# A planned encoder layer: tile places by end of last use, four rounds of planning, another transfer model

## The chip, the core and the metric

The kernel runs on one core of one Trainium2 chip. The metric is the device time of one execution in microseconds (us); before the change the median of three runs is 1985.77 us (1983.18 to 1986.04). Engines are named as in the profile: PE is TensorE, PEld its weight loads, DVE is VectorE, ACT is ScalarE, POOL is GpSimd, SP is SyncE, which here issues nearly all DMAs.

## What is computed

The reference is one layer of an encoder, for 1024 tokens of one new stream and 32 tokens of a running one (1056 together), with 1024 channels, in float32:

```python
def swiglu(x, w_gate, w_up, w_down):
    return (jax.nn.silu(x @ w_gate) * (x @ w_up)) @ w_down

def layer(x, ...):
    x = x + 0.5 * rmsnorm(swiglu(rmsnorm(x, g1a), f1g, f1u, f1d), g1b)
    m, k_new, v_new, h_last, new_buf = mixer(rmsnorm(x, gma), ...)
    x = x + rmsnorm(m, gmb)
    x = x + 0.5 * rmsnorm(swiglu(rmsnorm(x, g2a), f2g, f2u, f2d), g2b)
```

The two feed-forward nets (FFN1, FFN2) have 2816 = 22 x 128 inner channels. The mixer projects to queries, keys, values and two inputs of a recurrent block. Four heads of differential attention (two score maps each; the running stream also sees 512 cached keys) stand beside a causal convolution with a gated linear recurrence (RG-LRU) over 512 channels; both results are concatenated and projected once more.

## The kernel before

**Tiling.** Every float32 factor is split into a high and a low part of the type fp32r (a cast and a subtraction, `split`), and a product is made of three matmuls (`mm3`): high by high, high by low, low by high. The FFNs run in three stages. *Gate and up*: 11 rounds, each for two of the 22 blocks of inner channels. A round loads two 512 KB tiles of gate weights (`raw<-in_w1g`; `in_w2g` in FFN2) and two of up weights (`raw<-in_w1u`), forms the sums that a Strassen-like scheme of seven products needs (`left_operands`, tiles `W`, `s`, `raw`), multiplies them with the tiles `X` into PSUM (`pq`), combines the products in tiles `p` and `u`, and stores combinations of the result `H` to DRAM (`t_d<-H`). *Down*: tiles `traw` come back from `t_d`, become `T`, and are multiplied with the down weights (`pd`, `pe`). *Boundary*: `rstd` gets the norm. The sums of squares `acc` are added over the partitions by matmuls (`st<-ones,acc`), GpSimd raises them to the power -0.5 (tile `ms`), and matmuls with the identity spread them (`st<-ident,ms`).

In the mixer `pp` are the products of the input projection, `xc` and `th` the convolution's tiles, `pg` the products of the gates of the recurrence, which DVE computes by scans (`th<-lx,xc`). `KS` holds the cached keys, split in two parts. `Sh0s` to `Sh3s` and `Sh0q` to `Sh3q` are scores of head 0 to 3 for the running and the new stream, `pth2q`, `tpsh2q` and `oh2q` are transposed weights and outputs of head 2, `cat` the concatenated result, which goes through DRAM (`cat_d`), and `po` the products of the output projection with its weights `w` (high) and `wl` (low).

**Places.** SBUF is not given out by names but by rings. A `Ring` is a row of equal places; `S`, the largest, has 45 places of 1064 floats and holds the raw weights, `W`, `X`, `u`, `H`, `T` and most of the mixer's tiles. Three more rings hold `tp`, `up` and `acc` tiles, five the tiny ones. Each new tile takes a place by `Planner.take`, and its first writer has to wait until all users of the place's former holder are done.

**Order.** The program is run once without issuing anything: every operation becomes an `Op` with the engines that may do it and a cost on each. `Planner.run` takes places and finds the dependences, and then makes 12 passes. In a pass, `forward` fills the engines in the order of priorities by a model of costs; in it all transfers share one channel, each taking its bytes divided by 360 per ns behind a start of 1150 ns, and being usable 900 ns after that. `backward` runs the same from the end and gives the priorities of the next pass. The pass with the shortest modelled time decides the order and, where several engines may do an operation, the engine. `pin` then fixes this order on every engine, and the program is run again and issued (L138 before, L142 after, is the line that issues everything, so all rows of the profile name it). On the chip each engine and SP's DMA queue work in that order, and an instruction that waits holds those behind it.

Of the kernel before, what the change touches and what calls it, by code (L numbers as in the profile page):

```python
# [29 lines left out]
LOUD = 0  # L30
# [18 lines left out]
class Planner:  # L49
# [6 lines left out]


    ENGINES = ("tensor", "vector", "scalar", "gpsimd", "sync")
    PASSES = 12

    def __init__(self, tc, plan=None):
        self.tc, self.plan = tc, plan
        self.made = []
        self.count = 0
        self.floor = 0.0
        self.hurry = 0.0
        self.top = 0
        self.held = []
        self.old = {}
        self.cells_of = {}  # L70
        self.last_use = {}
        self.events = []
        self.slots = []
        self.ops = []
        self.deps = []
        self.cells = {}
        self.touched = {}
        for e in self.ENGINES:
            setattr(self, e, EngineView(self, (e,)))
        self.adder = EngineView(self, ("vector",))  # L80
        self.copier = EngineView(self, ("scalar", "vector"), (0, 0))
        self.later = EngineView(self, ("vector",))
# [20 lines left out]
    def take(self, name, ring):  # L103


        now = len(self.deps)
        found = [(self.last_use.get(t, -1), j) for j, t in enumerate(ring.holds)]
        last, j = min(found)
        assert last < now, (ring.name, name)
        ring.holds[j] = name  # L110
        self.slots.append(j)
        _, space, lo = ring.slots[j]
        hi = lo + ring.size
        waits, keep = {}, []
        for sp, a, b, other in self.held:
            if sp == space and a < hi and lo < b:
                found = [u for cell in self.cells_of.get(other, ()) for users in self.cells[cell].values() for u in users]
                waits.update(dict.fromkeys(found) if found else self.old[other])
                keep += [(sp, *g, other) for g in ((a, lo), (hi, b)) if g[0] < g[1]]
            else:  # L120
                keep.append((sp, a, b, other))
        self.held = keep + [(space, lo, hi, name)]
        self.old[name] = waits
# [64 lines left out]
    def forward(self, prio):  # L188

        ops, n = self.ops, len(self.ops)  # L190
        left = [len(d) for d in self.deps]
        est = [op.floor for op in ops]
        end, start, chosen = [0.0] * n, [0.0] * n, [None] * n
        free = dict.fromkeys(self.ENGINES, 0.0)
        later = {e: [] for e in self.ENGINES}
        ready = {e: [] for e in self.ENGINES}
        order = {e: [] for e in self.ENGINES}
        dma, table, skip = 0.0, None, set()
        window, worked, cold = 0, 0.0, True

        def release(i):
            for e in ops[i].engines:
                heapq.heappush(later[e], (est[i], prio[i], i))

        for i in range(n):
            if not left[i]:
                release(i)
        todo = n
        while todo:
            best = None  # L210
            for e in self.ENGINES:
                q, r = later[e], ready[e]
                while r and chosen[r[0][1]] is not None:
                    heapq.heappop(r)
                while q and (q[0][0] <= free[e] or chosen[q[0][2]] is not None):
                    _, p, i = heapq.heappop(q)
                    if chosen[i] is None and (i, e) not in skip:
                        heapq.heappush(r, (p, i))
                t = free[e] if r else q[0][0] if q else None
                if t is not None and (best is None or t < best[0]):  # L220
                    best = (t, e)
            t, e = best
            q, r = later[e], ready[e]
            while q and q[0][0] <= t:
                _, p, i = heapq.heappop(q)
                if chosen[i] is None and (i, e) not in skip:
                    heapq.heappush(r, (p, i))
            if not r:
                continue
            p, i = heapq.heappop(r)  # L230
            if chosen[i] is not None:
                continue
            op = ops[i]
            if len(op.engines) > 1:
                k = op.engines.index(e)
                mine = t + op.costs[k] + op.bias[k]
                other = [max(free[o], est[i]) + op.costs[j] + op.bias[j] + sum(ops[x].cost(o) for _, x in ready[o][:8] if x != i and _ < p)
                         for j, o in enumerate(op.engines) if j != k and (i, o) not in skip]
                if other and min(other) < mine:
                    skip.add((i, e))  # L240
                    continue
            cost = op.cost(e)
            if e == "tensor":
                while t >= (window + 1) * GATE:
                    cold = worked < (0.8 if cold else 0.4) * GATE
                    window, worked = window + 1, 0.0
                cost *= 1 + cold
                worked += cost * (op.writes[0].free_size() > 1)
            if op.tables:
                if table not in op.tables:  # L250
                    table = op.tables[0]
                    cost += 1300
            chosen[i] = e
            start[i] = t
            free[e] = t + cost
            if op.size:
                dma = max(t + 1150, dma) + op.size / 360.0
                end[i] = dma + 900
            else:
                end[i] = t + cost  # L260
            order[e].append(i)
            todo -= 1
            for j, kind in self.after[i]:
                d = ops[j]
                if kind == ORDER:
                    x = start[i]
                elif op.size:
                    x = end[i]
                else:
                    x = end[i] + (0 if len(d.engines) == 1 and d.engines[0] == e and (e == "tensor" or kind == AGAIN) else LATENCY[e][d.engines[0]])  # L270
                est[j] = max(est[j], x)
                left[j] -= 1
                if not left[j]:
                    release(j)
        return chosen, start, end, order, max(end)

    def backward(self, prio, chosen):

        ops, n = self.ops, len(self.ops)
# [10 lines left out]
        while todo:  # L290
            best = None
            for e in self.ENGINES:
                q, r = later[e], ready[e]
                while q and q[0][0] <= free[e]:
                    _, p, i = heapq.heappop(q)
# [14 lines left out]
            for j, kind in self.deps[i].items():  # L310
                o = ops[j]
                if kind == ORDER:
                    x = t + cost - o.cost(chosen[j])
                elif o.size:
                    x = t + cost + o.size / 360.0 + 1600
                else:
                    x = t + cost + (0 if chosen[j] == e and (e == "tensor" or kind == AGAIN) else LATENCY[chosen[j]][e])
                est[j] = max(est[j], x)
# [2 lines left out]
                    heapq.heappush(later[chosen[j]], (est[j], prio[j], j))  # L321
        return at

    def run(self):
        for f, args in self.events:
            f(*args)
        n = len(self.ops)
        self.after = [[] for _ in range(n)]
        for i, deps in enumerate(self.deps):
            for j, kind in deps.items():  # L330
                self.after[j].append((i, kind))
        best = None
        prio = list(range(n))
        for k in range(self.PASSES):
            found = self.forward(prio)
            if LOUD:
                print("pass", k, found[4])
            if best is None or found[4] < best[0][4]:
                best = found, prio
            chosen, start = found[:2]  # L340
            prio = [-a - op.hurry for op, a in zip(self.ops, self.backward([-s for s in start], chosen))]
        best, _ = best
        self.chosen, self.start, _, self.order, _ = best
        self.ops = self.deps = self.after = self.cells = self.events = None

    def pin(self):
# [16 lines left out]
class Op:  # L363
    def __init__(self, engines, bias, name, args, kw, floor):
# [11 lines left out]
            self.bias = bias[:k] + bias[k + 1:]  # L376
        self.size, self.tables = 0, None
        if name == "dma_start":
            side = self.writes[0] if self.writes[0].space != bass.MemoryType.DRAM else self.reads[0]
            self.size = side.free_size() * side.shape[0] * 4  # L380
        elif name == "activation":
            self.tables = TABLES.get(args[2])
        self.costs = [engine_cost(e, self) for e in self.engines]
# [5 lines left out]
class Ring:  # L389


    def __init__(self, plan, stack, name, size, bufs, banks=None):
        self.plan, self.name, self.size = plan, name, size
        self.holds = [None] * (len(banks) if banks else bufs)
        if banks is not None:
            self.slots = banks
            return
# [1169 lines left out]
```

## Time and profile before

| | before |
|---|---|
| median of 3 runs | 1985.77 us (1983.18 to 1986.04) |
| the profiled execution's own time | 1988.15 us |
| its span, first to last instruction | 1986.4 us |
| mean granted clock of TensorE | 0.987 |
| PE / DVE / ACT / POOL busy | 1899.0 / 1444.8 / 642.5 / 70.1 us |
| bytes read / written in HBM | 157.48 / 65.83 MB |

The time of an execution is a little longer than the span of its instructions. A duration in the trace is that of the profiled execution. Matmuls of TensorE overlap, so the distance between their starts tells what one costs, not the duration of one.

### The profile page before, as it was taken

The page shows a single profiled execution, that of the slowest core. Times are in us where ns is not written, and L with a number is a line of the kernel's source. Part 1 is how long each engine was busy: PE and PEld are TensorE (multiplying, and loading weights), DVE is VectorE, ACT ScalarE, POOL GpSimd, SP SyncE. Part 2 cuts the span into 40 slices and gives each one's busy share as a digit, 9 for nine tenths or more (in the row PEclk, how much of TensorE's full clock was granted, in tenths as well). Part 3 has the DMA queues.
Part 4 walks back from the last instruction along what each step waited for, and adds up shares of the span by engine and source line. Part 5 has one row for each costly group of instructions (what it writes and reads, how often), then busy time and mean ns, then how long its engine had stood idle before and what let it go on. Part 6 is the DMA issues. An engine that isn't in the chain of part 4 may idle for free.

```text
span 1986.4 us, 35224 instructions
## 1 busy us (share of the span) xinstructions
PE 1899.0 (96%) x14456; PEld 1850.0 (93%) x14456; DVE 1444.8 (73%) x2649; ACT 642.5 (32%) x1259; POOL 70.1 (4%) x79
## 2 busy tenths in 40 slices
PE   5999999999999999997998899989999999999997
PEld 5999999999999999896987789989999999999997
DVE  7867677676789588257677868797677676778857
ACT  5311111113332144164377763341111211223212
POOL 2000000000000011002000010000000000000000
PEclk9999999999999999998999999989999999999998
DMA  3223233234554253242433432232233222464442
GB/s 131 82 92 92 87 119 98 90 94 154 178 164 137 82 160 100 78 141 92 129 89 103 127 120 86 88 103 92 87 118 98 88 96 82 159 208 142 148 120 88
DMA packets 127809, 225.60 MB, mean 114 GB/s; under 512 B 11424, under 2 KB 84896, under 8 KB 127648
## 3 DMA queue, kind: packets, MB, share of 16 engines
q1 hardware_dynamic: 127504, 223.31, 35.5%
q8 instruction: 113, 1.85, 0.4%
q14 instruction: 48, 0.39, 0.1%
q10 hardware_dynamic: 144, 0.05, 0.0%
HBM read 157.48 MB, written 65.83 MB: 112 GB/s over the span
## 4 chain that ended last, share of the span: by engine, by line
PE 72%; DVE 13%; DMA 8%; ACT 3%; issue 3%; POOL 1%; SPq 1%; POOLq 0%; DVEq 0%; ACTq 0%
PE pq L138 31%; PE pd L138 19%; PE pp L138 7%; PE pe L138 4%; PE po L138 4%; PE pv L138 3%; DVE W L138 2%; DVE H L138 2%; DMA raw<-in_w1u 2%; DVE raw L138 1%; DMA raw<-in_w2u 1%; PE st L138 1%; DVE y L138 1%; DMA t_d<-H 1%; DVE u L138 1%
## 5 line engine op out<-in xcount | busy, mean ns | idle before, releaser
L138 PE MATMUL pq<-X,W 128*128 128x264 f32 x7488 | 931.1, 286 | 18.9 <-DVE u L138 10.6
L138 PEld LDWEIGHTS pq<-X,W 128*128 128x128 f32 x7488 | 922.5, 190 | 24.6 <-DVE u L138 14.5
L138 PE MATMUL pd<-T,W 128*128 128x264 f32 x3024 | 368.7, 284 | 0.0
L138 PEld LDWEIGHTS pd<-T,W 128*128 128x128 f32 x3024 | 368.3, 188 | 0.0
L138 ACT CAST W<-raw 128x512 fp32r<-128x512 f32 (+1 forms) x226 | 133.8, 607 | 511.5 <-DVE raw L138 233.1
L138 DVE TENSOR_TENSOR W<-raw,W 128x512 fp32r<-128x512 f32 (+1 forms) x376 | 246.3, 670 | 13.9 <-ACT W L138 10.9
L138 DVE TENSOR_TENSOR u<-u,pq 128x528 f32<-128x528 f32 x80 | 56.3, 704 | 101.0 <-PE pq L138 100.5
L138 PE MATMUL pp<-xm,w 128*128 128x352 f32 x384 | 127.5, 332 | 0.8 <-ACT w L138 0.8
L138 PE MATMUL pp<-xm,wl 128*128 128x352 f32 x384 | 125.9, 328 | 0.0
L138 DVE TENSOR_TENSOR raw<-raw 128x512 f32<-128x512 f32 (+1 forms) x150 | 115.0, 772 | 4.8 <-DMA raw<-in_w1d 2.0
L138 DVE TENSOR_TENSOR u<-p,pq 128x528 f32<-128x528 f32 x80 | 56.2, 702 | 84.8 <-PE pq L138 84.8
L138 ACT CAST T<-traw 128x528 fp32r<-128x528 f32 x84 | 52.2, 634 | 172.9 <-DMA traw<-t_d 110.9
L138 DVE TENSOR_TENSOR T<-traw,T 128x528 fp32r<-128x528 f32 x126 | 85.8, 704 | 4.9 <-ACT T L138 3.5
L138 POOL TENSOR_TENSOR ms<-ms,neghalf 128x3 f32<-128x3 f32 x24 | 31.6, 1320 | 1518.2 <-DVE ms L138 1518.2
L138 DVE CAST W<-raw 128x512 fp32r<-128x512 f32 (+1 forms) x150 | 62.2, 416 | 28.4 <-ACT H L138 12.1
L138 DVE TENSOR_TENSOR acc<-acc,sq 128x264 f32<-128x264 f32 x167 | 69.6, 429 | 13.2 <-ACT sq L138 11.2
L138 PE MATMUL po<-cat,wl 128*128 128x264 f32 x256 | 73.3, 290 | 4.5 <-DVE wl L138 4.5
L138 PE MATMUL po<-cat,w 128*128 128x264 f32 x256 | 76.4, 303 | 1.0 <-ACT y L138 0.5
L138 PEld LDWEIGHTS pp<-xm,w 128*128 128x128 f32 x384 | 73.1, 190 | 2.6 <-ACT w L138 1.1
L138 PEld LDWEIGHTS pp<-xm,wl 128*128 128x128 f32 x384 | 72.9, 190 | 1.0 <-DVE wl L138 0.6
L138 PE MATMUL pe<-h,w 128*128 128x264 f32 x256 | 73.2, 286 | 0.0
L138 PE MATMUL pe<-hl,w 128*128 128x264 f32 x256 | 73.1, 286 | 0.0
(410 smaller groups left out, 2549.3 us busy)
## 6 DMA issues: line engine op xcount, KB each, us to landing
t_d<-H SPq DMA_DIRECT2D x126, 264.0 KB, 2.3
traw<-t_d SPq DMA_DIRECT2D x56, 528.0 KB, 3.9
raw<-in_w1g SPq DMA_DIRECT2D x22, 512.0 KB, 3.6
raw<-in_w1u SPq DMA_DIRECT2D x22, 512.0 KB, 4.2
raw<-in_w2u SPq DMA_DIRECT2D x22, 512.0 KB, 3.8
raw<-in_w2g SPq DMA_DIRECT2D x22, 512.0 KB, 3.6
raw<-in_w1d SPq DMA_DIRECT2D x36, 256.0 KB, 3.7
raw<-in_w2d SPq DMA_DIRECT2D x36, 256.0 KB, 3.5
```

What stands on the lines that cost most here:

```text
L138: self.made.append(f(*args, **kw).ins)
```

## The change

No operation of the computation is added, removed or resized. Three things change in the planner.

*Which place.* `take` took the place whose holder has its last use first in the order of the program text. Now the first of four rounds does that; in the next rounds it takes, among the places whose holder has no later use in the program, the one whose holder's last use ends earliest in the schedule that the former round found (`self.left`). Each round makes the places and the dependences anew (`replay`) and has 6 passes, and the best of all passes counts, together with its places (`slots`).

*Transfers.* One byte in the model takes 1/305 ns in place of 1/360, and 1.5 times that where the tile has at most 64 partitions, and again 1.5 times where the rows on the far side have at most 128 elements. A load is usable 1000 ns behind its last byte and a store 400 ns, where both had 900.

*Tables.* A table load of ACT counts 1410 ns in place of 1300.

```diff
-    PASSES = 12
+    ROUNDS, PASSES = 4, 6
...
         now = len(self.deps)
         found = [(self.last_use.get(t, -1), j) for j, t in enumerate(ring.holds)]
-        last, j = min(found)
-        assert last < now, (ring.name, name)
+        found = [(self.left.get(ring.holds[j], 0.0) if self.left else last, j) for last, j in found if last < now]
+        assert found, (ring.name, name)
+        j = min(found)[1]
...
-                    cost += 1300
+                    cost += 1410
...
-                dma = max(t + 1150, dma) + op.size / 360.0
-                end[i] = dma + 900
+                dma = max(t + 1150, dma) + op.moved
+                end[i] = dma + op.landing
...
-                    x = t + cost + o.size / 360.0 + 1600
+                    x = t + cost + o.moved + 700 + o.landing
...
+        for k in range(self.ROUNDS):
+            self.replay()
+            mine = None
+            for n in range(self.PASSES):
+                found = self.forward(prio)
...
+                if mine is None or found[4] < mine[4]:
+                    mine = found
...
+            if best is None or mine[4] < best[0][4]:
+                best = mine, self.slots
+            self.left = {}
+            for op, end in zip(self.ops, mine[2]):
+                for ap in op.reads + op.writes:
+                    self.left[ap.tensor.name] = max(end, self.left.get(ap.tensor.name, 0.0))
+            prio = mine[1]
...
-            side = self.writes[0] if self.writes[0].space != bass.MemoryType.DRAM else self.reads[0]
+            side, far = self.writes[0], self.reads[0]
+            self.landing = 1000
+            if side.space == bass.MemoryType.DRAM:
+                side, far, self.landing = far, side, 400
             self.size = side.free_size() * side.shape[0] * 4
+            self.moved = self.size / 305.0 * (1.5 if side.shape[0] <= 64 else 1) * (1.5 if far.ap[-1][1] <= 128 else 1)
```

What the diff doesn't tell is how the order moves. Three places show it.

SP's queue in the first rounds of FFN1's gate and up stage, before (behind the loads of the input `x`; the first round's weights are loaded ahead of these):

```order
L138 DMA x<-in_xt 128x2x264 x12
L138 DMA t_d<-H 128x2x264
L138 DMA raw<-in_w1u 128x1024
L138 DMA t_d<-H 128x2x264
L138 DMA raw<-in_w1u 128x1024
L138 DMA raw<-in_w1g 128x1024 x2
L138 DMA t_d<-H 128x2x264 x5
L138 DMA raw<-in_w1g 128x1024 x2
L138 DMA t_d<-H 128x2x264 x2
L138 DMA raw<-in_w1u 128x1024
L138 DMA t_d<-H 128x2x264
L138 DMA raw<-in_w1u 128x1024
```

The same place of SP's queue after:

```order
L142 DMA x<-in_xt 128x2x264 x12
L142 DMA raw<-in_w1g 128x1024
L142 DMA t_d<-H 128x2x264 x2
L142 DMA raw<-in_w1g 128x1024
L142 DMA raw<-in_w1u 128x1024 x2
L142 DMA t_d<-H 128x2x264 x5
L142 DMA raw<-in_w1g 128x1024 x2
L142 DMA raw<-in_w1u 128x1024
L142 DMA t_d<-H 128x2x264
L142 DMA raw<-in_w1u 128x1024
L142 DMA t_d<-H 128x2x264 x6
```

The second round's loads moved ahead of stores, and in the rounds that follow the first load of up weights stands next to the gate weights, and six stores follow each other where four and two stood.

DVE's order at the first use of the cached keys (`KS`) in the mixer, before:

```order
L138 TENSOR_TENSOR xc<-xc,th 128x1060
L138 SCALAR_TENSOR_TENSOR th<-a_9745,th 128x352
L138 SCALAR_TENSOR_TENSOR th<-lx,xc 128x1024
L138 SCALAR_TENSOR_TENSOR th<-lx,cst,xc 128x32
L138 TENSOR_TENSOR xc<-xc,th 128x1060 x3
L138 SCALAR_TENSOR_TENSOR th<-lx,xc 128x1024
L138 SCALAR_TENSOR_TENSOR th<-lx,cst,xc 128x32
L138 SCALAR_TENSOR_TENSOR th<-lx,xc 128x1024
L138 SCALAR_TENSOR_TENSOR th<-lx,cst,xc 128x32
L138 TENSOR_TENSOR KS<-u,KS 64x512
```

And after (the rows with `th<-lx` are the scans, long ones for the new stream and short ones for the running one):

```order
L142 TENSOR_TENSOR xc<-xc,th 128x1060
L142 SCALAR_TENSOR_TENSOR th<-a_9745,th 128x352
L142 SCALAR_TENSOR_TENSOR th<-lx,xc 128x1024
L142 CAST KS<-u 128x512
L142 SCALAR_TENSOR_TENSOR th<-lx,cst,xc 128x32
L142 SCALAR_TENSOR_TENSOR tq<-pp,rb 128x352
L142 CAST KS<-u 128x512
L142 TENSOR_TENSOR KS<-u,KS 64x512 x2
```

Two scan pairs and the three `xc` sums moved behind `KS`, and its casts moved from ACT to DVE. Between the last `pg` product and the first `Sh0s` PE has 92 `pp` products before and 76 after.

PE's order where the attention of head 2 ends and the output projection begins, before:

```order
L138 MATMUL Sh3s<-KS,Q 32x512
L138 MATMUL Sh3s<-KS,Ql 32x512
L138 MATMUL tpsh2q_11852<-ident,P0h2q_11839 128x128
L138 MATMUL tpsh2q_11852<-ident,P0h2q_11822 128x128
L138 MATMUL tpsh2q_11852<-ident,P0h2q_11839 128x128
L138 MATMUL tpsh2q_11861<-ident,P0h2q_11839 128x128 x2
L138 MATMUL po<-cat_11996,w 128x264
```

And after:

```order
L142 MATMUL Sh3q_12190<-K,Q 128x512
L142 MATMUL Sh3q_12190<-K,Ql 128x512
L142 MATMUL Sh3q_12198<-K,Q 128x512
L142 MATMUL Sh3q_12198<-K,Ql 128x512
L142 MATMUL Sh3q_12198<-K,Q 128x512
L142 MATMUL po<-cat_11996,w 128x264
L142 MATMUL po<-cat4l,w 128x264
L142 MATMUL Sh3q_12198<-K,Ql 128x512
```

Scores of head 3 moved ahead of the first `po`. From the last `pp` to the first `po` there are 36 matmuls before and 61 after, and of the `po` products 310 before and 256 after stand ahead of the last output of head 3. At FFN2's entry the last norm's sums stand 93 `pq` products behind the norm ahead of it before and 114 after, and 3 and 16 `pq` products lie between its sums and its `st<-ident,ms`.

## Rows read from the trace of the kernel before

**Rows 1.** The page, part 1: busy us (share of the span) xinstructions.

```profile
PE 1899.0 (96%) x14456; PEld 1850.0 (93%) x14456; DVE 1444.8 (73%) x2649; ACT 642.5 (32%) x1259; POOL 70.1 (4%) x79
```

**Rows 2.** Stretches: us, busy PE, PEld, DVE, ACT, POOL (xinstructions), PEclk, DMA share, GB/s.

```profile
0.00:35.00 35.00, 14.42 (x61) 13.57 (x62) 24.86 (x73) 19.63 (x47) 8.98 (x9) 1.00 0.54 185
76.00:90.00 14.00, 11.43 (x80) 11.04 (x79) 10.84 (x25) 4.57 (x9) 0.00 (x0) 0.88 0.50 175
90.00:504.00 414.00, 408.53 (x3332) 406.36 (x3331) 291.15 (x479) 88.34 (x146) 0.00 (x0) 1.00 0.32 102
504.00:737.00 233.00, 233.00 (x1923) 233.00 (x1921) 180.58 (x314) 68.41 (x139) 2.90 (x3) 1.00 0.46 141
737.00:760.00 23.00, 19.72 (x124) 18.78 (x124) 22.43 (x50) 13.67 (x30) 5.29 (x12) 0.93 0.71 244
...
990.00:1125.00 135.00, 119.81 (x687) 103.44 (x686) 104.39 (x249) 98.27 (x204) 8.00 (x10) 0.96 0.42 122
...
1225.00:1330.00 105.00, 96.33 (x748) 94.11 (x748) 87.85 (x185) 40.42 (x86) 8.20 (x6) 0.95 0.26 84
1330.00:1738.00 408.00, 402.52 (x3287) 400.67 (x3286) 290.54 (x473) 86.25 (x143) 0.00 (x0) 1.00 0.32 104
...
910.00:919.40 9.40, 0.33 (x3) 0.04 (x2) 9.34 (x11) 2.08 (x3) 9.05 (x6) 0.70 0.21 62
919.40:930.00 10.60, 9.07 (x35) 6.83 (x36) 9.75 (x17) 4.02 (x6) 2.46 (x2) 0.62 0.54 152
```

**Rows 3.** Waits of PE, whole span: waiting op <- op waited for, sum us, times, longest.

```profile
PE st L138 <- POOL ms L138: 12.5, 5, 4.6
PE pq L138 <- DVE u L138: 10.6, 14, 1.8
PE Sh0s L138 <- DVE KS L138: 9.4, 2, 9.1
```

**Rows 4.** Timeline of SP, 70 to 84 us: start, us, engine, op, out<-in, count.

```profile
73.54 0.39 SPq L138 DMA_DIRECT2D t_d<-H  x1
...
76.31 1.67 SPq L138 DMA_DIRECT2D raw<-in_w1g  x2
```

**Rows 5.** Waits of PE in 90 to 480 us, and in 1330 to 1725 us.

```profile
PE pq L138 <- DVE u L138: 4.3, 8, 1.3
...
PE pq L138 <- DVE u L138: 4.5, 4, 1.8
```

**Rows 6.** Timeline of SP, 1635 to 1650 us.

```profile
1643.21 4.94 SPq L138 DMA_DIRECT2D t_d<-H  x2
1648.64 0.34 SPq L138 DMA_DIRECT2D raw<-in_w2u  x1
```

**Rows 7.** Timeline of DVE, 1647 to 1666 us; [idle before <-releaser].

```profile
1654.68 0.69 DVE L138 TENSOR_TENSOR W<-raw,W 128x512 fp32r<-128x512 f32 x1 [1.97 <-ACT W L138]
...
1659.41 0.43 DVE L138 CAST W<-s 128x512 fp32r<-128x512 f32 x1
```

**Rows 8.** Timeline of DVE, 900 to 925 us.

```profile
907.91 2.29 DVE L138 TENSOR_TENSOR_SCAN th<-lx,xc 128x1024 f32<-128x1024 f32 x1
910.11 0.26 DVE L138 TENSOR_TENSOR_SCAN th<-lx,cst,xc 128x32 f32<-128x32 f32 x1
910.29 3.58 DVE L138 TENSOR_TENSOR xc<-xc,th 128x1060 f32<-128x1060 f32 x3
...
918.66 0.69 DVE L138 TENSOR_TENSOR KS<-u,KS 64x512 fp32r<-64x512 f32 x1
```

**Rows 9.** Timeline of PE, 1091.5 to 1092.5 us: two products `pp`.

```profile
1091.77 0.32 PE L138 MATMUL pp<-xm4l,w 128*128 128x352 f32 x1
1091.93 0.32 PE L138 MATMUL pp<-xm,wl 128*128 128x352 f32 x1
```

**Rows 10.** DMA issues: op, count, KB each, median us from issue to landing.

```profile
t_d<-H SPq DMA_DIRECT2D x126, 264.0 KB, 2.3
...
raw<-in_w1d SPq DMA_DIRECT2D x36, 256.0 KB, 3.7
```

More of the change, by code (lines that the diff above doesn't have):

```diff
@@ L64, in __init__ @@
         self.count = 0
+        self.left = None
+        self.rings = []
         self.floor = 0.0
@@ L322, in backward, with replay @@
         return at
-    def run(self):
+    def replay(self):
+        for ring in self.rings:
+            ring.holds = [None] * len(ring.holds)
+        self.held, self.old, self.cells_of, self.slots = [], {}, {}, []
+        self.deps, self.cells, self.touched = [], {}, {}
         for f, args in self.events:
             f(*args)
-        n = len(self.ops)
-        self.after = [[] for _ in range(n)]
+        self.after = [[] for _ in self.ops]
         for i, deps in enumerate(self.deps):
@@ L331, in run @@
                 self.after[j].append((i, kind))
+    def run(self):
         best = None
[L333 to L343, printed above, removed]
+        prio = list(range(len(self.ops)))
+        for k in range(self.ROUNDS):
[3 more added lines that the diff above has]
+                found = self.forward(prio)
+                if LOUD:
+                    print("pass", n, found[4])
+                if mine is None or found[4] < mine[4]:
+                    mine = found
+                chosen, start = found[:2]
+                prio = [-a - op.hurry for op, a in zip(self.ops, self.backward([-s for s in start], chosen))]
+            if best is None or mine[4] < best[0][4]:
[5 more added lines that the diff above has]
+            prio = mine[1]
+        (self.chosen, self.start, _, self.order, _), self.slots = best
         self.ops = self.deps = self.after = self.cells = self.events = None
@@ L394, in __init__ @@
         self.holds = [None] * (len(banks) if banks else bufs)
+        plan.rings.append(self)
         if banks is not None:
```

## The prediction

> **What bounds the kernel now.** I read the page's busy shares first. TensorE is busy for 1899.0 of 1986.4 us, VectorE, the next one, for 73% [rows 1]. So a change of order can only win what TensorE doesn't work: 1986.4 - 1899.0 = 87.4 us of idle time, and the time that it works at the lower of its two clocks. Then I read the stretches, to see where these lie [rows 2]. The down stage from 504 to 737 us is covered whole, and the two gate/up loops (90 to 504, 1330 to 1738) lack 414.0 - 408.5 = 5.5 us each. The idle time sits in the first 35 us (20.6), at 76 to 90 (2.6), 737 to 760 (3.3), around 910 to 930 (10.6), in the attention heads from 990 to 1125 (15.2) and at the entry to the second FFN, 1225 to 1330 (8.7). Each short stretch also shows a granted clock under 1: at 2.4 GHz it would read 1.00, a stretch wholly at 1.2 GHz 0.50, so 0.88 over 14 us is 3.4 us at half clock, and 1.7 us of work lost. Last, the waits of TensorE by what ended them [rows 3]: DVE's `u` 14 times, `KS` once for 9.1 us, the norms' `ms` from GpSimd. No row shows TensorE held by the arithmetic that the change leaves alone, and the change takes no arithmetic away. It is worth what it does to these places.
>
> **What the change does, in order's terms.** It changes three things: which tile place is taken, what the planner believes of transfers, and how many passes it makes. Only the resulting order reaches the chip. I go by the places where TensorE waits.
>
> **1. First to second round of gate and up.** Now, the last weight load that the second round needs stands behind a store of `H`: SP waits for DVE's `H`, issues the store at 73.54, then, among others, both `w1g` at 76.31 [rows 4]. TensorE waits for DVE's `W`, made of that load. Afterwards one `w1g` is issued ahead of every store, the other and both `w1u` behind two stores; so the load that is now sixth in line comes first. I take the whole stall and the clock loss behind it away: -2.6 - 1.7 = **-4.3 us** (bounds -4.3 and 0: 0 if the places of these loads come free as late as before).
>
> **2. The other rounds.** Here DVE's `u` ends the wait: 4.3 us over 8 waits in the first loop, 4.5 us over 4 in the second [rows 5]. The cause can be read from one: at 1643.21 SP spends 4.94 us on two stores of `H`, of which the second waits for DVE, and only then, at 1648.64, issues `w2u` [rows 6]. DVE then idles 1.97 us for the cast of that load, and its later work, the last `u` at its end, comes late [rows 7]. Afterwards the first up load goes out right behind the gate loads, with no store between them, and only the second keeps one store ahead. DVE's chain is then without the 1.97 us, which is more than the longest of the waits (1.8). I take 7 of 4.3 + 4.5 = 8.8 us: **-7 us** (bounds -8.8, and 0 as the second load keeps its store).
>
> **3. The cached keys, at 910 us.** TensorE waits 9.07 us for the first `KS` tile. DVE does three sums `xc` (3.58 us) and two more scans between the first scan and `KS` [rows 8]. Afterwards only two casts, one short scan and one `tq` stand there. A cast of 512 columns took DVE 0.43 us [rows 7], the short scan 0.26, and `tq` with its 352 columns at most the 0.69 of `KS` with 512 [rows 8]. From the start of the first scan to the end of `KS` that is 2.29 + 0.43 + 0.26 + 0.69 + 0.43 + 0.69 = 4.8 us, where it is now 918.66 + 0.69 - 907.91 = 11.4: `KS` comes 6.6 us earlier. Against that TensorE has 76 instead of 92 `pp` products ahead of it, 16 x 0.16 us = 2.6 us less cover [rows 9]. The stall becomes 9.07 - 6.6 + 2.6 = 5.1, so -4.0 us. Of the clock, 0.62 over 10.6 us behind the stall [rows 2] is 8 us at half clock, 4 us of lost work; since a stall of 2.6 us was enough for the half clock at 84 us, I expect most of that loss to stay and take 1 off. Sum **-5 us** (bounds -13.1, stall and clock loss both gone, and 0, as the casts that DVE now takes wait for the loads of the cached keys, which no row here times against them).
>
> **4. Heads 1 to 3.** The stretch lacks 15.2 us, and at 0.96 over 135 us it spends 10.8 us at half clock, at most 5.4 us lost [rows 2]. Two moves pull against each other. Between the last `pp` and the first `po` stand 61 matmuls instead of 36; the added 25 are scores of the last head, brought forward: 25 x 0.16 = 4 us of work where the waits for `pth2q`, `cat2l` and `wl` now fall. But only 256 instead of 310 `po` products run before attention is over: 54 x 0.12 = 6.5 us less to fill its later waits (0.12 being 233.0 us over 1923 matmuls of the same 264 columns [rows 2]). I take **0** (bounds -8, about half of idle time and clock loss, and +8, the 6.5 and some clock behind it).
>
> **5. Entries at 737 and 1225 us.** Together 3.3 + 8.7 us idle, and 0.93 of 23 and 0.95 of 105 us [rows 2] are 3.2 and 10.5 us at half clock, at most 6.9 us lost. At the second FFN's entry the last norm now has 16 instead of 3 `pq` products (1.6 us) between its sums and the use of their power from GpSimd, which fits the waits for `ms` [rows 3]; but its sums stand 114 - 93 = 21 products later in the row and other norms lost cover. I take **-2** for both entries (bounds -10 and +4, one more wait of the size of the longest `ms` there).
>
> **6. What is new.** Weight loads, their places and the DVE/ScalarE split of casts move everywhere, also in stretches that are now covered whole. No row prices a wait that isn't there; the nearest is the longest in the loops, 1.8 us [rows 3]. I take two, **+3.6** (bounds 0 and +15, a 0.7 us wait, the loops' mean, at 20 rounds). The first 35 us change order a little and lack 20.6 us, all behind the input's load and the norm; I take 0 (bounds -2 and +2, the size of one wait for `ms`). The model's higher price of a table load and its new count of passes cost nothing on the chip, beyond the order.
>
> **How the numbers follow.** -4.3 - 7 - 5 + 0 - 2 + 3.6 = **-14.7 us** against the profiled execution's 1988.15, so 1973.4. That execution is 2.4 us above the median of 1985.77; on the median the forecast is **1971**.
>
> One constant of the new model can be weighed against the trace. It now counts 400 ns for the end of a store to DRAM and 1000 ns for a load, where both had 900. The rows bear it out: a 264 KB store of `H` lands 2.3 us after issue, a 256 KB load of `w1d` 3.7 us [rows 10]. The Trainium skill, "DMA: Bandwidth & Descriptors" (section "Latency and other measured facts"), says the reverse, that the receipt from the target dominates a transfer's fixed cost and that HBM is the slowest target; by it, a load that waits for a store (as at `cat_d`) would be planned too early, and the sum would be the 1.4 us between the two rows worse. The row decides; the sum above is without it.
>
> **Rivals.** *Given back*: the loop's waits only change their name. The gate loads now stand behind six stores of `H` in place of four, so `W` may become the late one; with step 2 at 0 and step 6 at +6 the sum is -4.3 + 0 - 5 - 2 + 6 = -5.3, about 1980, and with step 3 halved 1983. For it: DVE works 291 of 414 us in the loop and ScalarE 88 [rows 2], but the wait there is one of order, not of capacity, which speaks for another order to remove it. *Slower*: the same queue as one mechanism. SP is in order; a load whose place is not free holds all stores behind it, DVE's next `H` tile then waits for its place, and the stall repeats in each of the 20 rounds. At the present longest wait of 1.8 us in each, that is 36 - 8.8 = +27, with the other steps' -11.3 a sum of +16: 2002. It decides where a load that is moved ahead of stores finds its place taken for longer than those stores now take. Against it: the place rule takes the earliest one to come free, and the loads move by two stores only. *More*: steps 4 and 5 gain half of their idle time as well, -8 and -8 more, and step 6 is nothing: 1953. *Does nothing*: that the model's finer numbers change the order without moving a wait; the two orders differ at every place read here, so I count this into the second.
>
> **Chances.** Forecast case, 1959 to 1978: 0.56. More, under 1959: 0.11. Given back, 1978 to 1990: 0.19, of which 0.08 lies below 1981.8. Slower, over 1989.7: 0.14. With 0.2% (4 us, about what a measurement here can tell from no change) as the border, faster is 0.56 + 0.11 + 0.08 = 0.75, same 0.11, slower 0.14. The range leaves out most of the slower case and the far end of the better one: 1955 to 1988.
>
> **What would show it.** Step 1: no wait of TensorE for `W` near 82 us. Step 2: the waits for `u` under 2 us in all, and no gap of DVE behind the cast of an up load. Step 3: one wait for `KS` of about 5 us, half clock behind it. Step 4: idle time at 990 to 1125 within 8 us of 15.2. Step 6 is wrong if a covered stretch (504 to 737 us) shows idle time. The prediction is wrong as a whole if waits for `W` or `raw` appear in most rounds of the loops.

## The result

The changed kernel takes 1956.8 us (median of 4 runs, 1952.6 to 1959.8) against 1985.9 us of the kernel before, a ratio of 0.985 (95% interval 0.982 to 0.988). The forecast was 1971, within 1955 to 1988: the direction was right, the gain of 29 us is twice the one forecast, and the time lies near the lower end of the range. The profiled execution took 1959.79 us, with a span of 1958.0.

The page of the changed kernel, part 1, answers to [rows 1]: TensorE works as long as before (1897 us), so what went is time in which it waited.

```profile
PE 1897.3 (97%) x14456; PEld 1853.7 (95%) x14456; DVE 1417.7 (72%) x2612; ACT 656.2 (34%) x1292; POOL 62.2 (3%) x79
```

Stretches of the changed kernel, columns as in [rows 2]. They are cut at the same events as in the table below: the 672nd `pq`, the first `pd`, the first `pg`, the first `Sh0s`, the last `oh0q`, FFN2's first `pq`, and so on.

```profile
0.00:120.41 120.41, 100.77 (x720) 99.26 (x721) 96.96 (x209) 48.90 (x97) 7.05 (x10) 0.99 0.30 100
120.41:491.70 371.29, 371.29 (x3051) 371.29 (x3049) 251.72 (x413) 89.74 (x150) 0.00 (x0) 1.00 0.34 106
491.70:855.21 363.51, 360.19 (x2614) 349.66 (x2613) 257.49 (x449) 101.21 (x203) 16.30 (x29) 0.99 0.40 131
855.21:911.73 56.52, 51.73 (x315) 49.99 (x313) 40.47 (x80) 43.80 (x60) 0.42 (x2) 1.00 0.49 137
911.73:990.27 78.54, 76.05 (x450) 68.65 (x451) 61.35 (x131) 32.33 (x82) 8.37 (x10) 0.98 0.43 124
990.27:1221.91 231.64, 218.96 (x1442) 198.34 (x1441) 170.65 (x409) 144.12 (x335) 19.39 (x19) 0.96 0.33 100
1221.91:1333.74 111.83, 106.17 (x855) 105.06 (x853) 98.63 (x197) 46.28 (x95) 6.36 (x5) 0.98 0.32 99
1333.74:1705.55 371.81, 371.49 (x3050) 371.28 (x3049) 251.41 (x408) 86.62 (x146) 0.00 (x0) 1.00 0.33 105
1705.55:1892.07 186.52, 186.52 (x1538) 186.52 (x1537) 144.19 (x228) 48.03 (x85) 0.00 (x0) 1.00 0.52 169
```

Both loops are now covered: 371.29 of 371.29 us, and 371.49 of 371.81. The same stretches beside those of before; "half clock" is half of TensorE's busy time within the stretches granted 1.2 GHz, so the work lost there:

| stretch | width, us | idle, us | half clock, us |
|---|---|---|---|
| start and first round | 120.6 → 120.4 | 23.2 → 19.6 | 1.7 → 1.7 |
| FFN1 loop | 379.6 → 371.3 | 5.5 → 0.0 | 0 → 0 |
| down stage, entry to the mixer, projection | 356.3 → 363.5 | 3.3 → 3.3 | 1.7 → 4.9 |
| first `pg` to last `oh0q` | 142.7 → 135.1 | 13.7 → 7.3 | 3.2 → 1.5 |
| heads 1 to 3, to FFN2's first `pq` | 237.5 → 231.6 | 15.9 → 12.7 | 4.7 → 8.9 |
| entry to FFN2, first round | 117.9 → 111.8 | 8.5 → 5.7 | 3.9 → 1.7 |
| FFN2 loop | 378.9 → 371.8 | 5.5 → 0.3 | 0 → 0 |
| FFN2 down stage | 186.9 → 186.5 | 0 → 0 | 0 → 0 |
| tail | 66.0 → 65.9 | 11.8 → 11.8 | 0.7 → 0.7 |
| span | 1986.4 → 1958.0 | 87.4 → 60.7 | 16.0 → 19.4 |

So 26.7 us of idle time went, 3.5 us of clock loss came, and 5.2 us were gained that both traces show as busy, 4.8 of them in the two loops. (`pp` and `po` products moved across the borders in the middle of the table, so there the widths alone say little.) The waits of TensorE in the changed kernel, columns as in [rows 3]:

```profile
PE st L142 <- DVE acc L142: 9.3, 2, 9.1
PE st L142 <- POOL ms L142: 6.6, 4, 2.5
PE pq L142 <- ACT p L142: 4.7, 2, 2.5
PE pp L142 <- DVE y L142: 2.8, 1, 2.8
...
PE pp L142 <- DVE tq L142: 2.3, 1, 2.3
...
PE Sh0s L142 <- DVE KS L142: 0.4, 1, 0.4
...
PE pq L142 <- DVE u L142: 0.3, 1, 0.3
```

The 14 waits for `u` are down to one of 0.3 us, and `KS` from 9.1 to 0.4. New are two waits for `p`, a copy on ScalarE, and one each for `y` and for `tq`.

### The profile page after: what moved, and what is told of

The parts are those of the page before. It is cut to its first block, busy times and chain, and to the rows that moved or that the text cites. A ratio compares the mean times of both kernels' runs of the same rounds, so it can differ in the third digit from the quotient of the medians.

```text
span 1958.0 us, 35215 instructions
## 1 busy us (share of the span) xinstructions
PE 1897.3 (97%) x14456; PEld 1853.7 (95%) x14456; DVE 1417.7 (72%) x2612; ACT 656.2 (34%) x1292; POOL 62.2 (3%) x79
## 5 line engine op out<-in xcount | busy, mean ns | idle before, releaser
L142 PEld LDWEIGHTS pq<-X,W 128*128 128x128 f32 x7488 | 921.8, 190 | 12.7 <-ACT p L142 5.1
L142 ACT CAST W<-raw 128x512 fp32r<-128x512 f32 (+1 forms) x251 | 147.7, 601 | 433.3 <-PE pq L142 269.7
L142 ACT CAST T<-traw 128x528 fp32r<-128x528 f32 x75 | 45.3, 633 | 118.6 <-DMA traw<-t_d 96.1
L142 PE MATMUL pe<-h,wl 128*128 128x264 f32 x256 | 72.7, 286 | 0.0
```

Source lines behind the costliest of these rows:

```text
L142: self.made.append(f(*args, **kw).ins)
```

## The experiments

**Queue or place?** My step 2 said that a store ahead of the load on SP's queue holds it up. The traces show another candidate. SP's queue in one FFN1 round, of before and then of after:

```profile
160.08 4.92 SPq L138 DMA_DIRECT2D t_d<-H  x2
165.17 0.34 SPq L138 DMA_DIRECT2D raw<-in_w1u  x1
166.55 0.36 SPq L138 DMA_DIRECT2D t_d<-H  x1
168.19 0.34 SPq L138 DMA_DIRECT2D raw<-in_w1u  x1
```

```profile
142.28 0.34 SPq L142 DMA_DIRECT2D raw<-in_w1g  x1
158.77 0.33 SPq L142 DMA_DIRECT2D raw<-in_w1u  x1
159.38 0.38 SPq L142 DMA_DIRECT2D t_d<-H  x1
161.76 0.33 SPq L142 DMA_DIRECT2D raw<-in_w1u  x1
```

The planner's list of places tells what the places of these raw tiles held. Before, it was weights `W` of the up round before, read by TensorE in the sixth and in the last of its seven products; the last matmuls that read them end at 165.04 and 168.09, and the loads go out at 165.17 and 168.19. So it is with all 36 up loads of the two loops' last nine rounds: each is issued 0.03 to 0.43 us behind the last read of its place. Afterwards the first takes the place of a raw gate tile, which is free once DVE has made its last `W` of it (158.74, issue 158.77), and the second that of weights of the fifth product (last read 161.73, issue 161.76): both come some two products earlier. To tell queue from place, the kernel before got the changed order on SP's queue, and kept its places:

```diff
+    def ahead(self):
+        row = self.order["sync"]
+        for k in range(2, len(row)):
+            load, one, two = (self.ops[i] for i in (row[k], row[k - 1], row[k - 2]))
...
+                row[k - 2:k + 1] = row[k], row[k - 2], row[k - 1]
```

> The kernel before with its places, engines and orders, but on SP's queue, in every round of the two gate/up loops, the first load of up weights goes ahead of the two stores of H behind which it stood (as the changed kernel has it). Theory Q, the queue (step 2 of the prediction: the store ahead of the load delays it): the load is issued earlier, the waits of TensorE for u (5.5 us in each loop as shown) go, and the loops take 371 to 373 us in place of 379.6 and 378.9: about 1971. Theory P, the place (the load waits for its place, which holds weights that TensorE reads until the sixth of the seven products of the round before is done): the load is issued within 0.2 us of the same moment as before, the two stores come half a microsecond later, and the waits stay: 1986, within 2.

Measured: 2056.2 us, a ratio of 1.036 (1.033 to 1.038). Theory Q falls. P is right on the issue, and far off on what it costs. Of this run SP's queue in a round, its FFN1 loop, and the waits there:

```profile
259.39 0.33 SPq L138 DMA_DIRECT2D raw<-in_w1u  x1
259.81 0.39 SPq L138 DMA_DIRECT2D t_d<-H  x1
262.48 0.33 SPq L138 DMA_DIRECT2D raw<-in_w1u  x1
262.86 8.37 SPq L138 DMA_DIRECT2D t_d<-H  x6
```

```profile
117.37:530.64 413.27, 385.67 (x3050) 383.59 (x3049) 264.89 (x434) 80.61 (x133) 0.00 (x0) 0.96 0.31 97
```

```profile
PE pq L138 <- DVE u L138: 27.6, 9, 4.3
```

The load still goes out as its place comes free (last read 259.36, issue 259.39), but now all stores stand behind it. In eight of the nine rounds TensorE waits 2.7 to 4.3 us for `u`, where the longest wait was 1.8 (the ninth wait, at the loop's end, is 1.2), and it falls to half clock behind six of these eight; the loop takes 413.3 us in place of 379.6. The very queue order that costs 69 us with the old places is the one that the changed kernel runs without a wait.

**Place rule or transfer model?** Three kernels take the change apart: the old rule (one round of 12 passes) with the new model; the new rule for the raw tiles alone with the old model and with the new one.

```diff
-    ROUNDS, PASSES = 4, 6
+    ROUNDS, PASSES = 1, 12
```

> The changed kernel with one round of 12 passes, so with the old rule for places, and the new transfer and table model. Theory P (the place rule carries the loops): the loops keep their waits, 5 us or more shown in each, and the time falls by what the mixer and the entries gain at most: 1974 to 1988. Theory M (the transfer model carries it): the loops lose their waits, 371 to 373 us each, about 1957 to 1965.

```diff
-        found = [(self.left.get(ring.holds[j], 0.0) if self.left else last, j) for last, j in found if last < now]
+        found = [(self.left.get(ring.holds[j], 0.0) if self.left and name.startswith('raw') else last, j) for last, j in found if last < now]
```

(and, in the first of the two, 360 bytes per ns, 900 ns and 1300 ns as before)

> The old transfer and table model, and the new place rule (four rounds) for the raw tiles alone, which the loads write; all other tiles by the old rule. Theory P: the loads of a round are issued ahead of its stores, the waits for u go, and both loops fall to 371 to 373 us: 1986 - 15 = 1971, within 5, since the rest of the program moves too. Theory M: no gain in the loops, 1982 to 1990.

> The changed kernel with the new place rule for the raw tiles alone, the new transfer and table model. Theory P: loops of 371 to 373 us each, as in the changed kernel. If the raw tiles' places and the transfer model are all that matters, 1957 as the changed kernel, within 4; if places of the other tiles matter in the mixer and at its borders, the loops' 15 us alone, 1963 to 1972. Theory M doesn't tell it from the changed kernel.

Measured: 1984.4 us for the model alone (ratio 0.999, 0.997 to 1.001), 1974.1 for raw places with the old model (0.994, 0.992 to 0.996), 1969.4 with the new one (0.991, 0.989 to 0.994). The loops of the model alone, and of the raw places with the old model:

```profile
119.81:500.25 380.44, 375.22 (x3051) 373.46 (x3050) 263.71 (x436) 80.84 (x132) 0.00 (x0) 1.00 0.32 104
1353.27:1730.77 377.50, 373.62 (x3051) 371.81 (x3049) 261.56 (x427) 77.92 (x129) 0.00 (x0) 1.00 0.33 105
```

```profile
117.05:493.48 376.43, 372.25 (x3051) 371.61 (x3050) 252.21 (x408) 93.05 (x155) 0.00 (x0) 1.00 0.34 108
1346.77:1720.31 373.54, 371.99 (x3050) 371.34 (x3049) 251.59 (x402) 90.41 (x152) 0.00 (x0) 1.00 0.34 108
```

Without the place rule the loops stay at 380.4 and 377.5 us: theory M falls. With it for the raw tiles alone they come to 376.4 and 373.5 with the old model and to 374.3 and 373.7 with the new one, 0.5 to 5 us longer than I expected. Three waits for `u` are left in each loop of the former, and five in all in the latter.

A late load doesn't explain what is left. Of the raw places with the old model, the waits of TensorE, the up loads of one FFN1 round, and a later row of ScalarE in that round:

```profile
PE pq L142 <- DVE u L142: 5.7, 6, 1.7
```

```profile
188.88 7.77 SPq L142 DMA_DIRECT2D raw<-in_w1u  x2
```

```profile
216.57 0.62 ACT L142 CAST W<-raw 128x512 fp32r<-128x512 f32 x1 [7.24 <-PE pq L142]
```

The round's first matmul starts at 198.88, so its two up loads (188.88 and 196.33) go out 10.0 and 2.6 us ahead of the round; the changed kernel issues them 2.5 us ahead of it and 0.4 us into it, the kernel before 3.2 and 6.2 us into it. TensorE still idles 1.29 us for `u` at 218.58. DVE makes this `u` behind a `W` that waits for the cast at 216.57, and the cast starts as a product of TensorE ends (216.56). A cast of raw weights takes no data from TensorE, so what it waits for is the place of its own tile `W`, which the old rule chose. Then the complement, the new rule for all tiles but the raw ones:

```diff
+        ... self.left and not name.startswith('raw') ...
```

> The complement of the run with raw places: the new place rule for all tiles but raw, new transfer and table model. Theory P (a load of a round waits for the place of its raw tile): the loops keep waits of 4 us or more each, 376 to 381 us. For the keys: if the places of other tiles make the short KS stall of the changed kernel, it is under 3 us here as there, and the time 1968 to 1976; if it takes both, the stall stays at 9 to 16 us and the time 1976 to 1985.

Measured: 1972.3 us (0.991, 0.990 to 0.993). Its loops:

```profile
119.83:491.43 371.60, 371.45 (x3051) 371.24 (x3049) 256.05 (x421) 84.00 (x141) 0.00 (x0) 1.00 0.33 105
1344.51:1717.57 373.06, 371.72 (x3050) 371.07 (x3049) 256.21 (x415) 82.31 (x139) 0.00 (x0) 1.00 0.33 105
```

So theory P, as I had put it, is wrong too: the raw tiles need not choose for themselves. With all others placed by the schedule, what is left for the up loads are the places of the fifth and the sixth product's weights, one product (24 matmuls of 0.12 us, 2.9 us) earlier than before, and that already exceeds the longest wait of 1.8 us. So an earlier load helps, but the earliest load does not give the shortest loop: the complement issues its loads later than the raw places do and waits less, and the places of the tiles that are made from a load count as well. Of 10.6 us of waits for `u` the raw places leave 5.7 (4.5 with the new model), the other places 2.5, and both together 0.3. For the keys, the complement's stall (4.1 us, see below) is neither of the two that I had named, and its time lies in the range of the shorter one. What stays open: where the waits go, DVE also has 8 to 12 us less work in a loop (casts went to ScalarE, 264 to 252 us), about the size of the waits; no run held the split fixed. Less DVE work alone doesn't do it: in FFN1's loop the raw places have 252 us of it and keep 4.2 us of idle time, where the complement has 256 and 0.15.

**What is the 9 us stall of the keys?** The kernel before with step 3 alone: on DVE's row both `KS` go right behind the first pair of scans. The second run moves the low part of the query, `Ql`, as well.

```diff
+    def ahead(self):
+        row = self.order["vector"]
+        keys = [i for i in row if self.ops[i].name == "tensor_sub" and self.ops[i].writes[0].tensor.name.startswith("KS")][:2]
...
+        k = row.index(after) + 1
+        self.order["vector"] = row[:k] + keys + row[k:]
```

> The kernel before, with step 3 alone: on DVE's row the first two KS go from behind three xc sums and two pairs of scans to right behind the first pair; places, engines and all else stay. ScalarE's casts end at 911.5, so the first KS should be ready at about 911.8 in place of 919.35 and the stall of 9.07 us become 1.5 to 2. Theory A (the stall is worth itself, nothing stands late behind it): -7 us and up to 2 us of clock, 1977 to 1980. Theory B (given back: the sums and scans that now come later are the next wait, or the maxima mn of head 0's scores are): 1983 to 1987, with the 7 us found again as waits between 912 and 1000 us.

> The run with the keys alone, with the low part of the query (Ql) moved as well: on DVE's row of the kernel before, KS, Ql, KS go right behind the first pair of scans. In the run with the keys alone Sh0s then waited 8.6 us for Ql, which had stayed behind the sums and scans. Theory A (the stall is worth itself once all that DVE owes the scores is ahead): the stall of 9 us falls under 2 us, 1977 to 1980. Theory B (the next of DVE's late results takes it, as Ql did): 1983 to 1988, and a new wait of 4 us or more between 912 and 1000 us.

Measured: 1987.0 us (0.999, 0.998 to 1.001) and 1986.0 us (1.000, 0.998 to 1.001): nothing, theory B. The waits of TensorE in the first and in the second run:

```profile
PE Sh0s L138 <- DVE Ql L138: 8.6, 1, 8.6
```

```profile
PE pp L138 <- ACT w L138: 10.2, 1, 10.2
```

First `Ql` takes the stall, as it had stayed behind the scans; then `w`, weights of the projection. In the second run SP issues the load of these weights at 920.74, as a scan on DVE ends (rows of DVE, then SP):

```profile
920.46 0.26 DVE L138 TENSOR_TENSOR_SCAN th<-lx,cst,xc 128x32 f32<-128x32 f32 x1
```

```profile
920.74 0.35 SPq L138 DMA_DIRECT2D raw<-in_win  x1
```

By the plan the load's place held `lx`, which that scan reads last. In the kernel before the same scan ends at 916.27 and the load goes out at 916.29; in the changed one, where the place held weights of an earlier projection, it goes out at 902.94, ahead of the scans. Rows of the kernel before (SP, then ScalarE), then SP of the changed one:

```profile
916.29 0.34 SPq L138 DMA_DIRECT2D raw<-in_win  x1
920.64 1.05 ACT L138 CAST w<-raw 128x1024 fp32r<-128x1024 f32 x1 [8.16 <-DMA raw<-in_win]
```


```profile
902.94 0.33 SPq L142 DMA_DIRECT2D raw<-in_win  x1
```

So a place holds this load in the kernel before. That the changed kernel gains by its early load is not shown, and the runs above speak against the load as the whole cause. With raw tiles placed by the new rule and the old model, the last load of `in_win` ahead of the scores goes out at 883.08, and TensorE still waits 10.8 us for `KS`, which stands behind three pairs of scans on DVE; the cast of these weights waits for DVE's `th`, which it doesn't read. The new model alone has a stall of 16.4 us, raw places with the new model 12.6. In the complement `KS` stands behind the first pair of scans, and its stall is 4.1 us though the load is late. ScalarE with raw places and the old model, then SP and ScalarE of the complement:

```profile
914.64 1.04 ACT L142 CAST w<-raw 128x1024 fp32r<-128x1024 f32 x1 [6.97 <-DVE th L142]
```

```profile
912.93 0.81 SPq L142 DMA_DIRECT2D raw<-in_win  x2
919.10 1.04 ACT L142 CAST w<-raw 128x1024 fp32r<-128x1024 f32 x1 [1.47 <-DMA raw<-in_win]
```

From the first `pg` to the last `oh0q` the complement idles 8.2 us, where the kernel before idles 13.7 and the changed one 7.3. So this gain comes with the new rule for the tiles other than raw, whose order has `KS` early; moving `KS` and `Ql` alone in the old order gives nothing. Which other part of that order it needs stays open.

**Do the model's numbers matter?** The changed kernel without the two factors of 1.5 and, in another run, with 900 ns of landing for loads and stores; the first of them and the changed kernel once more beside each other; and the first with six rounds of 12 passes.

```diff
-            self.moved = self.size / 305.0 * (1.5 if side.shape[0] <= 64 else 1) * (1.5 if far.ap[-1][1] <= 128 else 1)
+            self.moved = self.size / 305.0
```

> The changed kernel without the two factors of 1.5 for narrow transfers (305 bytes per ns and the new landings stay). If the place rule carries the gain and the model's numbers only shuffle the rest: 1957, within 6, loops of 371 to 373 us. If the factors matter, it is in the mixer, where the narrow transfers are (keys, queries): loops the same, 1962 to 1972.

> The changed kernel with the old landing of 900 ns for loads and stores alike (305 bytes per ns and the factors stay). If the place rule carries the gain: 1957, within 6, loops of 371 to 373 us. If the store's shorter landing matters, it is where a load waits for a store (queries, keys, cat_d): loops the same, 1962 to 1972.

> The changed kernel again, beside the next run on the same chip: 1953 to 1960.

> The changed kernel without the two factors of 1.5, again. If they cost something, the 2.5 us between the first measurements come again (ratio to before lower by 0.001 or more); if they only shuffle, the two lie within 2 us of each other.

> As the run without the factors, with six rounds of 12 passes in place of four of 6, which lead to another order. The loops are already without waits, so what is left to gain is in the mixer and at its borders: 1948 to 1958. If the planner's model no longer tells the chip's differences at this size, it is as likely slower as faster than the run without the factors.

| kernel | median, us | ratio to before | interval |
|---|---|---|---|
| changed, first and again | 1956.8, 1956.0 | 0.985, 0.984 | 0.982 to 0.988, 0.982 to 0.986 |
| no factors, first and again | 1954.3, 1954.6 | 0.982, 0.983 | 0.980 to 0.983, 0.980 to 0.985 |
| old landing | 1953.6 | 0.981 | 0.980 to 0.983 |
| no factors, 6 rounds of 12 passes | 1951.6 | 0.981 | 0.979 to 0.983 |

With the place rule for all tiles, every variant of the model lands within about 5 us, with loops of 371 to 373 us as expected; the factors and the new landings bring nothing, and may cost 1 to 3 us, which the intervals don't separate. The last row is the fastest kernel of this study by its median; beside the changed kernel on the same chip its intervals still overlap. As for the passes: with 24 in place of 12 and all else old, the planner finds the same order as before, and with three or eight rounds the same as with four. No run has the place rule for all tiles with the whole old model, since in the plan to which it leads engines wait for one another without end; its effect is read from the runs with a part of the tiles or a part of the model. The rate of 305 bytes per ns and the 1410 ns of a table load were not taken back alone.

## The prediction, step by step

The time lies in the case *More* (under 1959, chance 0.11), but not for that case's reasons: it wanted the idle time of steps 4 and 5 to fall by half. (Its 1953 takes -8 for each of these two steps; -8 on top of their 0 and -2 would give 1951.) Of the 13.7 us by which the span fell beyond 14.7, the loops account for 8.5, the new waits that did not come for 3.6 and the keys for 2.6, against 4.1 missing in step 1 and 1.0 in step 4; about 4 are not put down to a step. That the time stayed inside the range is partly luck, as the cause given for the largest term was wrong.

**1, the second round (-4.3): wrong.** The loads do go out earlier, yet TensorE waits 2.3 us in place of 2.6, at half clock as before, and the stretch takes 120.4 us in place of 120.6. What is late now is `p`. Rows of ScalarE in the changed kernel:

```profile
86.02 0.62 ACT L142 CAST W<-raw 128x512 fp32r<-128x512 f32 x1 [3.54 <-DVE W L142]
86.55 0.59 ACT L142 COPY p<-pq 128x528 f32<-128x528 f32 x1
```

The copy that frees the bank stands behind a cast that waited 3.54 us for DVE. The step failed in that it took the whole stall away and named nothing behind the load.

**2, the loops (-7): right in direction, wrong in its cause, half the size.** They gained 8.3 + 7.1 = 15.5 us. The cause is the place, not the store ahead on the queue [rows 6]: that SP spent 4.94 us on two stores and then issued the load was true, but the load was not held by them. The size has two terms. I took 7 us of the waits shown, and 10.3 of 10.6 went. And a wait costs more than the trace shows as idle: the matmuls of a loop start 0.121 us apart and are recorded about 0.28 us long, so a late one shows as idle only behind the recorded end. Over the 3048 starts of the FFN1 loop the ten waits for `u` amount to 7.1 us of delay, where 5.5 us are shown as idle, 0.16 us each; with the smaller delays that show no idle time, 8.15 us. In the changed kernel no start in this loop is late.

**3, the keys (-5): -7.6 in the stretch from the first `pg` to the last `oh0q`, and not by the move that I costed.** Idle time there fell by 6.4 us and the clock loss by 1.7. The stall for `KS` went nearly whole (0.4 us, I had said 5.1), with a new wait of 2.3 us for `tq` right ahead of it. But the two runs that move what DVE owes the scores gained nothing, so my sum, which costed that move, does not explain it. What it left out is that the weights that `pp` needs next came as late as the keys: in the kernel before their cast ends at 921.7, 2.3 us behind the first `KS`. What in the new order brings the gain is open.

**4, the heads (0): right.** Idle time fell by 3.2 us and 4.2 us more were lost at half clock. (The traces record 42 and 73 matmuls from the last `pp` to the first `po`, 31 more and not 25; the 0 does not hang on it.) **5, the entries (-2): right in sum, -1.9,** though the entry to the mixer lost 3.1 us at half clock behind the wait for `y`, and FFN2's entry gained 5.0. **6, new waits (+3.6): too high.** The down stages stay covered; the waits that are new (`p`, `y`, `tq`) fall into the places of steps 1, 3 and 5 and are counted there. What is left of the 28.4 us, about 4, is time between the loops that both traces show as busy; I can't put it down to single waits.

Of the rivals, *slower* is the one that teaches most: loads ahead of stores on an in-order queue, each held by its place. It priced the stall at 1.8 us a round, 2002 us in all; the run that makes it happen shows 2.7 to 4.3 us in eight rounds of FFN1's loop, half clock behind most of them, and 2056 us. The changed kernel runs the same queue order without it, as its places come free earlier.

## What to carry over

Ask of a late load first which tile held its place and when that tile's last reader ends; compare that moment with the issue in the trace. If they agree to a few tenths of a microsecond, suspect the place: here moving the load ahead in its queue only held up what stood behind it, and other places helped. Then ask the same of the tiles that are made from the load. When one late instruction is moved ahead, look at what the stalled engine needs next, since two or three things may be late together.

## What the runs showed of the hardware

Waits of 2.7 to 4.3 us, one in nearly every round, cost more than themselves: in the queue run's FFN1 loop TensorE idles 27.6 us and loses another 13.0 us at 1.2 GHz (granted clock 0.96 over 413 us); in the loop of the kernel before, with waits of up to 1.3 us, the granted clock is 1.00. And with matmuls recorded longer than their distance, the idle time in a trace is a lower bound: 5.5 us shown, 8.2 us lost in the FFN1 loop of the kernel before.
